# A hybrid attention layer: the pacing count is zeroed with each change of pace, and the latent heads and first output products take a background step at every third tile

## The chip, the core and the metric

The kernel runs on one core of a Trainium2 chip. The metric is device time in microseconds for one execution, lower is better; the time before is the median of three runs. One execution was also recorded by the hardware profiler, and all durations in this document come from that record.

## What is computed

One layer with two groups of eight heads each. The latent heads (MLA, "m") take queries, keys and values from two normalised latent vectors of 768 and 512 columns, with a rotary part; the forgetting heads (FoX, "f") take them from the input directly and add a cumulated log of a forget gate to the scores. Both outputs are gated, joined, projected and normalised.

```python
h = _rms_norm(x, g_pre)                       # x: 512 tokens x 2048
proj = h @ w_in                               # all first projections in one matrix
q_lat, kv_lat, k_rope_raw, gate_mla, fq, fk, fv, f_logit, gate_fox = jnp.split(proj, ...)
o_mla = _mla_branch(q_lat, kv_lat, k_rope_raw, g_q, w_uq, g_kv, w_ukv, cos, sin) * silu(gate_mla)
o_fox = _fox_branch(fq, fk, fv, f_logit, b_forget) * silu(gate_fox)
o = jnp.concatenate([o_mla, o_fox], axis=-1) @ w_out
return x + _rms_norm(o, g_post)
```

Every matrix is float32. The kernel splits each operand into a high and a low part and multiplies three times (high by high, high by low, low by high; `mm3`, L137 to L140).

## The kernel before

**Chunks and tiles.** Weights come in chunks of at most 128 x 1024 float32 (512 KB), in an order fixed when the program is written down. `chunk(i)` issues the loads on SyncE's queue (SP) up to chunk i+4 (`load`, L221 or L230, into one of three `raw` buffers), and divides up to chunk i+2 (`divide`, L242 and L243: ScalarE copies `whi`, VectorE subtracts `wlo`; three buffers of each). A chunk is used in two or four *tiles*: one slice of 128 rows, with 6 or 9 matmuls of 512 columns, or as many columns in narrower ones.

**Stages, in order.** Forgetting heads in four pairs; one chunk group for the last latent columns (`lat`, 16 tiles); the other latent columns ("l") and the latent heads' gate ("m") as block products; the latent heads in four pairs (`for p in range(4)`, each with 6 tiles of w_uq and 4 of w_ukv); the output projection as block products, last the norm. While one pair of heads is projected, the scores and values of the pair before are put in between, taken from a queue `todo` (`pump`), one or two at each tile.

**Block products.** The gate, the latent columns and both halves of the output projection use seven products in place of eight of half the size (a Strassen-like scheme, `p1 p2 p4 q6 g5 g7 g3`). Four of the seven multiply not blocks of the weights but sums of blocks, t4 to t7. Each product has four chunks and eight tiles. The order for the output half is p1 (columns 0), p1 (columns 1), p2 (0), p4 (0), p4 (1), q6 (0), g5 (0) and so on, so that the first sums are used in the fourth product.

**The background sums.** The sums are made in DRAM while other work runs. The list `bg` has 64 entries: 32 for w_in, then 32 for w_out (16 for each half; their tensors are t4 to t7 and stand as `t` in the profile where a second number was in the name). `add_step(n, mark)` (L281 to L292) does three things: on GpSimd's queue (POOL) a DMA that adds the second block onto entry n-1 (L287), on SP's queue a DMA that copies the first block into entry n (L290), and on SP's queue a *mark* of 64 bytes from the current chunk's `whi` into the head of entry n+1 (L292). The mark holds the copy of the next step back: copy n+1 writes over the place where mark n+1 has to land first, and the mark itself can't start before that `whi` is written. The addition waits for its copy, and a load of a sum waits for its addition. A `whi` buffer can be written again only when the mark that reads it is through.

**The pace.** `paced(w)` is called once per tile. It counts `state["tiles"]` up, and where the count has reached `state["pace"]` it takes the pace off the count and does one step. There are 66 steps, from -1 to 64. The pace is 6 at the start, 4 for `lat` (L1172), 1000 from the first block products on (L1238, no steps meant), 6 from product g5 of the gate (L1291), 2.5 from the latent heads (L1305) and 4 from the output products (L1473). Only the pace is set at these places; the count runs on. Ahead of the output's product p4 stands `assert state["step"] > len(bg)`.

**Who waits for whom.** Each engine and each queue works in order. SP's queue carries the loads of chunks, the copies, the marks, and the fetches of activations parked in DRAM (L892); a copy that waits for its mark holds back all loads behind it. The order within a queue is set when the program is built.

Of the kernel before, what the change touches and what calls it, by code (L numbers as in the profile page):

```python
# [63 lines left out]
def tile_hybrid_layer(  # L64
# [30 lines left out]
    def slot(name, dt=F32, shape=(P, 2, S)):  # L95

        return sp.tile(list(shape), dt, tag="s", name=name)
# [4 lines left out]
    def proj_bank(name):  # L102
        return bank("pj", name, 4)
# [142 lines left out]
    state = {"loaded": 0, "divided": 0, "tiles": 0, "turn": 0, "step": -1, "pace": 6}  # L246
# [217 lines left out]
            todo.popleft()()  # L464

    later = deque()

    def paced(w):

        if state["step"] <= len(bg):  # L470
            state["tiles"] += 1
            if state["tiles"] >= state["pace"]:
                state["tiles"] -= state["pace"]
                add_step(state["step"], w[0:1, 0, 0:16].bitcast(F32))
                state["step"] += 1
# [432 lines left out]
    def operand(n, of):  # L908
        def parts(kk, t):
            return [oper[n, of][kk // 2][:, x, kk % 2, t * P : (t + 1) * P] for x in range(2)]  # L910

        return parts

    def product(name, g, parts, o, first, last, rate=1, at=None, held=0, side=(), turned=False):


        side = deque(side)
        kk = 0

        def step(j, kk, t, hi, lo):  # L920
            if not turned:
                mm3(
                    o[t], *parts(kk, t), hi[:, j, :], lo[:, j, :], first and kk == 0, last and kk == 7,
                    skip_group_check=True,
                )
                return
            for f in range(2):
                c = slice((2 * t + f) * P, (2 * t + f + 1) * P)
                mm3(
                    o[t][:, f * HALF : (f + 1) * HALF], hi[:, j, c], lo[:, j, c], *parts(kk),  # L930
                    first and kk == 0 and f == 0, last and kk == 7, skip_group_check=True,
                )

        rng = list(prods[name, g])
        for i in rng[: len(rng) - held]:
            hi, lo = chunk(i)
            for j in range(2):
                if at is not None and kk == at[0]:
                    at[1]()
                for t in range(2):  # L940
                    step(j, kk, t, hi, lo)
                kk += 1
                pump(rate)
                paced(hi)
                if side and not held and kk % 2 == 0:
                    side.popleft()()
        w = [chunk(i, ahead=0) for i in rng[len(rng) - held :]]
        if w:
            side.popleft()()
        for t in range(2):  # L950
            for m in range(2 * len(w)):
                step(m % 2, kk + m, t, *w[m // 2])
            if w:
                finish(t, 2, o[t])
# [84 lines left out]
    for p in range(4):  # L1039
# [18 lines left out]
        else:  # L1058
# [5 lines left out]
            if "v" in c:  # L1064
                n = 2 if p == 1 else 3
# [103 lines left out]
        latents[i] = split(raw(i), f"ln{i}")  # L1169

    todo.append(rotary_key)
    state["pace"] = 4  # L1172
    lb = [proj_bank(f"l4{i}") for i in range(2)]
    proj_T(lat, [(lb[i], P, two[i]) for i in range(2)], hh, hl)
    while later:
# [38 lines left out]
    def scaled(to, o, t0, add, op=ALU.add, col=hcol):  # L1214

        for t in range(2):
            dve.scalar_tensor_tensor(
                out=to[:, t, :], in0=o[t], scalar=col[:, t0 + t : t0 + t + 1], in1=add[:, t, :], op0=ALU.mult, op1=op
            )
# [5 lines left out]
    def gate(f, top, bottom):  # L1225

        if f % 2 == 0:
            o_of.append(slot(f"gm{f // 2}"))
        g = o_of[-1][:, f % 2, :]
        pt = att_bank(f"gmt{f}")  # L1230
        c = slice(f % 4 * P, (f % 4 + 1) * P)
        for t in range(NT):
            pe.transpose(pt[:, t * P : (t + 1) * P], (top, bottom)[t // 2][:, t % 2, c], ident)
        act.activation(g, pt, AF.Tanh)
        dve.scalar_tensor_tensor(out=g, in0=g, scalar=1.0, in1=pt, op0=ALU.add, op1=ALU.mult)
        gm.append(g)

    state["pace"] = 1000  # L1238
    A, A2 = ([proj_bank(f"g{n}{t}") for t in range(2)] for n in "lm")
    product("p1", "l", x_wide(0, 0), A, True, True, turned=True)  # L1240
    pl = slot("lp")
# [46 lines left out]
    product("q6", "m", operand("q6", "m"), C, True, True)  # L1288
    c12 = slot("gc12")
    scaled(c12, C, 0, pa, ALU.subtract)  # L1290
    state["pace"] = 6  # L1291
    product("g5", "m", operand("g5", "m"), G, True, True)
    c22 = slot("gc22")
    scaled(c22, G, 2, pb, ALU.subtract)
# [7 lines left out]
    todo.append(lambda: scaled(c12, G, 0, c12))  # L1302
    for f in range(4, 8):
        todo.append(lambda f=f: gate(f, c12, c22))
    state["pace"] = 2.5  # L1305
    for n in ("a11", "a12"):
        for f in fetches(n, "o"):
            f()
# [161 lines left out]
            square(t0 + t, c, o[t])  # L1470
            gain(t0 + t, c, o[t], homes.get(t0 + t))

    state["pace"] = 4  # L1473
    gps = [slot(f"gp{c}") for c in range(2)]

    def load_gp(c):
# [116 lines left out]
```

## Time and profile before

| | us |
|---|---|
| three runs | 961.98, 968.43, 968.26 |
| median | 968.26 |
| the profiled execution, device time | 962.62 |
| its span | 960.8 |

The profiled execution is 0.64 us above the lowest of the three runs and 5.64 below their median. TensorE (PE) is busy for 95% of the span. The profile's page cuts the span into 40 slices of 24.0 us and gives the busy share of each engine in tenths. The window view gives busy time, the number of instructions, the granted clock of TensorE as a share of full speed (PEclk), the mean busy share of the 16 DMA engines, and GB/s moved, for chosen stretches. The views of waits give who waited for whom: us in total, times, longest. Matmuls overlap: one of 512 columns takes 0.39 us and the next starts after less, so that the distance of two starts is what a matmul costs.

The stages in the trace, by the first start of their matmuls: `lat` 406.2, block products from 434.1, gate products q6 547.5, g5 560.1, g7 572.1; head pair 0 of the latent heads 631.5, pair 1 671.8, pair 2 about 713, pair 3 about 751; output products from 786.2, p4 from 832.4.

### The profile page before, as it was taken

How to read it: one execution, taken by the hardware profiler on the slowest of the kernel's cores; microseconds unless marked ns; L12 is line 12 of the kernel's file. 1: busy time of each engine (PE TensorE's matmuls, PEld its weight loads, DVE VectorE, ACT ScalarE, POOL GpSimd, SP SyncE). 2: the span in 40 equal slices, each digit the busy share in tenths (PEclk: the TensorE clock that was granted, in tenths of full speed). 3: DMA queues.
4: the chain of work that ended last, by engine and by line, in shares of the span. 5: the costliest groups of instructions: out<-in, count | busy, mean ns of one | idle time of the engine just before them, and what ended most of it. 6: DMA issues, size and time to landing. Idle time of an engine off the chain costs nothing.

```text
span 960.8 us, 12945 instructions
## 1 busy us (share of the span) xinstructions
PE 912.9 (95%) x4732; PEld 781.3 (81%) x4732; DVE 619.3 (64%) x1066; ACT 424.4 (44%) x779; POOL 87.5 (9%) x105
## 2 busy tenths in 40 slices
PE   8999999999999999999999995568899999999997
PEld 8988888988899888889999973347788888888885
DVE  4476886476634935737566775327588797796685
ACT  6762423243223422425645543214344456554474
POOL 0011101111200201111000001121100000000012
PEclk9999999999999999999999997689899999999999
DMA  9387988988988989897777689999921324777768
GB/s 291 86 234 200 233 207 224 226 202 226 255 200 216 214 233 246 206 219 254 241 243 250 191 255 246 250 262 246 233 78 35 107 89 155 239 232 242 263 200 248
DMA packets 122532, 203.60 MB, mean 212 GB/s; under 512 B 16194, under 2 KB 59740, under 8 KB 122468
## 3 DMA queue, kind: packets, MB, share of 16 engines
q1 hardware_dynamic: 105060, 158.85, 52.7%
q0 software_dynamic: 16672, 43.52, 24.2%
q8 instruction: 37, 0.61, 0.3%
q10 hardware_dynamic: 736, 0.40, 0.1%
q14 instruction: 27, 0.22, 0.1%
HBM read 190.66 MB, written 79.19 MB: 281 GB/s over the span
## 4 chain that ended last, share of the span: by engine, by line
PE 84%; DMA 12%; DVE 2%; SPq 1%; ACT 1%; issue 0%; ACTq 0%; DVEq 0%
DMA t<-whi 5%; PE fv L545 4%; DMA raw<-in_w_uq_dram 4%; PE fg L138 3%; PE fq L140 3%; PE fq L138 3%; PE fq L139 3%; PE fg L140 3%; PE fg L139 3%; PE fk L139 3%; PE fk L140 3%; PE fk L138 3%; PE sm L588 2%; PE fv L140 2%; PE fv L139 2%; PE fv L138 2%
## 5 line engine op out<-in xcount | busy, mean ns | idle before, releaser
L243 DVE TENSOR_TENSOR wlo<-raw,whi 128x1024 fp32r<-128x1024 f32 (+3 forms) x205 | 242.9, 1186 | 223.8 <-ACT whi L242 213.6
L242 ACT CAST whi<-raw 128x1024 fp32r<-128x1024 f32 (+3 forms) x205 | 209.4, 1022 | 337.2 <-PE fk L139 48.5
L138 PE MATMUL fq<-h,whi 128*128 128x512 f32 x128 | 52.6, 411 | 0.0
L138 PE MATMUL fg<-h,whi 128*128 128x512 f32 x128 | 50.9, 398 | 0.0
L140 PE MATMUL fq<-h,wlo 128*128 128x512 f32 x128 | 50.3, 393 | 0.0
L140 PE MATMUL fg<-h,wlo 128*128 128x512 f32 x128 | 50.1, 392 | 0.0
L139 PE MATMUL fq<-h,whi 128*128 128x512 f32 x128 | 50.1, 391 | 0.0
L138 PE MATMUL fk<-h,whi 128*128 128x512 f32 x128 | 50.0, 391 | 0.0
L139 PE MATMUL fg<-h,whi 128*128 128x512 f32 x128 | 49.9, 390 | 0.0
L139 PE MATMUL fk<-h,whi 128*128 128x512 f32 x128 | 49.8, 389 | 0.0
L140 PE MATMUL fk<-h,wlo 128*128 128x512 f32 x128 | 49.8, 389 | 0.0
L138 PE MATMUL mq<-ln,whi 128*128 128x512 f32 x72 | 30.6, 425 | 10.3 <-ACT whi L242 8.4
L140 PE MATMUL fv<-whi,h 128*128 128x256 f32 (+1 forms) x128 | 39.5, 309 | 0.0
L139 PE MATMUL fv<-wlo,h 128*128 128x256 f32 (+1 forms) x128 | 39.5, 309 | 0.0
L138 PE MATMUL fv<-whi,h 128*128 128x256 f32 (+1 forms) x128 | 39.5, 309 | 0.0
L545 PE MATMUL fv<-whi,h 128*128 128x456 f32 x128 | 37.7, 378 | 0.0
L287 POOL DMA_DIRECT2D t<-in_w_out_dram x16 | 19.4, 1302 | 154.9 <-DMA t<-in_w_out_dram 142.5
L139 PE MATMUL mq<-ln,whi 128*128 128x512 f32 x72 | 29.6, 411 | 0.0
L140 PE MATMUL mq<-ln,wlo 128*128 128x512 f32 x72 | 29.5, 413 | 0.0
L1409 POOL DMA_DIRECT2D c<-in_x_dram x8 | 7.1, 963 | 238.9 <-ACT c L1408 238.7
L605 ACT ACTIVATE pf<-sf,stf 128x128 f32<-128x128 f32 (+3 forms) x32 | 16.9, 528 | 26.9 <-DVE stf L603 26.9
L140 PEld LDWEIGHTS fq<-h,wlo 128*128 128x128 f32 x128 | 24.0, 188 | 5.4
(526 smaller groups left out, 2485.0 us busy)
## 6 DMA issues: line engine op xcount, KB each, us to landing
raw<-in_w_in_dram SPq DMA_DIRECT2D x80, 512.0 KB
t<-in_w_out_dram SPq DMA_DIRECT2D x32, 512.0 KB
raw<-t SPq DMA_DIRECT2D x32, 512.0 KB
raw<-in_w_out_dram SPq DMA_DIRECT2D x24, 512.0 KB
t<-in_w_out_dram POOLq DMA_DIRECT2D x16, 512.0 KB, 11.2
t<-t POOLq DMA_DIRECT2D x16, 512.0 KB, 8.1
awaymg<-rmg POOLq DMA_DIRECT2D x8, 512.0 KB, 7.7
raw<-in_w_ukv_dram SPq DMA_DIRECT2D x8, 512.0 KB
```

The costliest lines, as they stand in the source:

```text
L138: pe.matmul(o, ah, bh, start=first, stop=False, **kw)
L139: pe.matmul(o, ah, bl, start=False, stop=False, **kw)
L140: pe.matmul(o, al, bh, start=False, stop=last, **kw)
L242: act.copy(hi[:, :m], raw[:, :m])
L243: dve.tensor_tensor(out=lo[:, :m], in0=raw[:, :m], in1=hi[:, :m].bitcast(F32), op=ALU.subtract)
L287: pool.dma_start(to.rearrange("p (k c) -> p k c", k=2), second, accum_op=ALU.add)
L545: pe.matmul(banks[t][:, :n], a[k][:, tss[t]], b[:, j, :], start=k == 0 and m == 0, stop=k == NK - 1 and m == 2,)
L588: pe.matmul(s[:, :nn], a[:, qs], c[:, :nn], start=(i == 0), stop=(i == len(pairs) - 1))
L605: act.activation(p, s[:, :n], AF.Exp, bias=st[:, 0:1], accum_out=st[:, 1:2])
L1409: pool.dma_start(to, x[piece(t, c)], accum_op=ALU.add)
```

## The change

A helper sets the pace and the count together, and all changes of pace use it. The latent heads' pace goes from 2.5 to 3, that of the output products from 4 to 3.

```diff
     later = deque()
+
+    def set_pace(n):
+        state.update(pace=n, tiles=0)
...
-    state["pace"] = 4
+    set_pace(4)
     lb = [proj_bank(f"l4{i}") for i in range(2)]
...
-    state["pace"] = 1000
+    set_pace(1000)
     A, A2 = ([proj_bank(f"g{n}{t}") for t in range(2)] for n in "lm")
...
-    state["pace"] = 6
+    set_pace(6)
     product("g5", "m", operand("g5", "m"), G, True, True)
...
-    state["pace"] = 2.5
+    set_pace(3)
     for n in ("a11", "a12"):
         for f in fetches(n, "o"):
             f()
...
-    state["pace"] = 4
+    set_pace(3)
     gps = [slot(f"gp{c}") for c in range(2)]
```

No other line differs. What is computed, and every buffer, stays as it was.

## The prediction

> **What bounds the kernel now.** I read the page first. TensorE (PE) has work nearly everywhere, so time can be gained only where it has none.
>
> ```profile
> span 960.8 us, 12945 instructions
> PE   8999999999999999999999995568899999999997
> PE 84%; DMA 12%; DVE 2%; SPq 1%; ACT 1%; issue 0%; ACTq 0%; DVEq 0%
> ```
>
> The second line is PE's busy share in 40 slices of 24 us: one dip, 5 5 6 8 8, from about 600 us on. The third is the chain of waits that ended last: 84% PE, and 12% of the span (some 115 us) DMA. I cut that region by stages with the window view (columns: PE, weight load, VectorE, ScalarE and GpSimd busy with counts, granted clock, DMA share, GB/s):
>
> ```profile
> 406.00:434.00 28.00, 28.00 (x139) 23.18 (x138) 11.39 (x16) 8.83 (x16) 2.84 (x3) 1.00 0.92 213
> 572.00:631.00 59.00, 35.72 (x112) 24.90 (x111) 27.66 (x37) 17.50 (x23) 11.07 (x11) 0.74 1.01 248
> 631.00:672.00 41.00, 29.21 (x147) 23.40 (x146) 21.47 (x31) 13.71 (x27) 6.82 (x7) 0.92 1.06 263
> 672.00:713.00 41.00, 37.28 (x195) 31.80 (x194) 28.19 (x63) 17.64 (x45) 2.85 (x3) 0.92 0.72 175
> 713.00:751.00 38.00, 38.00 (x219) 32.81 (x217) 31.84 (x68) 19.38 (x50) 0.00 (x0) 1.00 0.20 60
> 751.00:786.00 35.00, 35.00 (x204) 30.78 (x203) 29.77 (x64) 17.59 (x43) 0.00 (x0) 1.00 0.23 76
> 786.00:805.00 19.00, 19.00 (x102) 15.83 (x100) 17.57 (x45) 12.09 (x31) 0.00 (x0) 1.00 0.36 112
> 805.00:822.00 17.00, 17.00 (x86) 14.01 (x85) 9.13 (x13) 9.92 (x17) 0.00 (x0) 1.00 0.62 199
> 822.00:832.00 10.00, 10.00 (x47) 8.30 (x46) 6.97 (x8) 5.43 (x8) 0.00 (x0) 1.00 0.87 292
> 832.00:854.00 22.00, 22.00 (x99) 18.22 (x98) 21.21 (x29) 14.90 (x22) 0.00 (x0) 1.00 0.72 217
> ```
>
> The second to fourth rows (gate products g7 and g3, then head pairs 0 and 1) are the dip. PE is idle for 23.3, 11.8 and 3.7 us there, and its clock is down to 0.74 and 0.92. The DMA engines are full, at 1.01 and 1.06. Right behind, in pairs 2 and 3, PE is full and DMA stands at 0.20 and 0.23. Who waits for whom between 572 and 672 us:
>
> ```profile
> PE gcm L138 <- ACT whi L242: 11.3, 3, 7.4
> PE mq L138 <- ACT whi L242: 8.4, 1, 8.4
> PE gdm L138 <- ACT whi L242: 8.3, 2, 7.2
> ACT whi L242 <- DMA t<-whi: 24.4, 9, 7.1
> SPq L290 <- DMA t<-whi: 41.3, 7, 9.6
> ```
>
> PE waits for divided weights, 28.0 us in these three rows. ScalarE, which divides, waits 24.4 us until a mark has read its buffer. SP waits 41.3 us at L290 with the loads queued behind it. So the background steps starve PE there, by filling the DMA engines.
>
> **Why they stand there: the count.** By the code, the forgetting heads have 14 groups of 16 tiles (q, k and g of four pairs, v of two). 224 tiles at pace 6 make 37 steps and leave 2. `lat` adds 16 at pace 4: 4 steps, 2 left. Eleven products of 8 tiles at pace 1000 raise the count to 90. At pace 6 each tile then adds one and takes six off, so a step falls on each of 18 tiles, and one more on the 24th. With 41 done, 60 of 66 are out when the latent heads begin, and the other 6 take 15 tiles at 2.5. The copies end in pair 1, as they should by this count:
>
> ```profile
> L290 SPq DMA_DIRECT2D t<-in_w_out_dram x32: 557/558/4197, 354.6 to 682.5; - x32
> 554.28 0.24 SPq L292 DMA_DIRECT2D t<-whi  x1
> 577.05 0.73 PE L138 MATMUL gcm<-whi,bmg 128*128 128x512 f32 x2 [1.41 <-ACT whi L242]
> ```
>
> (First row: min, median and max issue time in ns, then first and last start.) After the change `lat` still has 4 steps, each 2 tiles later, 41 in all. Then come 4 in products g5, g7 and g3 (24 tiles at 6), 13 in the latent heads (40 tiles at 3), and 8 in p1, p1 and p2 of the output (24 at 3). That is 66, the last on the last tile before the assertion.
>
> **Part 1: what goes.** What the dip would take with PE fed, from distances between starts:
>
> ```profile
> 841.70 0.39 PE L140 MATMUL ob<-whi,soa 128*128 128x512 f32 x1
> 849.86 0.39 PE L140 MATMUL ob<-whi,soa 128*128 128x512 f32 x1
> 545.81 0.28 PE L139 MATMUL gdl<-bmg,whi 128*128 128x256 f32 x1
> 547.37 0.28 PE L140 MATMUL gdl<-bmg,wlo 128*128 128x256 f32 x1
> 608.98 0.60 PE L1233 MATMUL gmt<-ident,gc 128*128 128x128 f32 x4
> PE mq L138 <- ACT mw L122: 1.9, 1, 1.9
> ```
>
> From 841.70 to 849.86 there are 36 distances: 0.227 us per matmul of 512 columns. From 545.81 to 547.37 there are 13: 0.12 us at 256. Products g7 and g3 have 16 tiles of 6: 96 x 0.227 = 21.8. Eight gates of four transposes: 8 x 0.60 = 4.8. Pair 0: 54 matmuls for w_uq and 24 for w_ukv, 78 x 0.227 = 17.7, and 48 narrow ones, 5.8. The wait for a bank in the last row, 1.9, stays. Sum 52.0 us, where the trace takes 572 to 672, 100 us: 48 gone. Pair 1 should take what pair 2 takes, 38 instead of 41: 3 more. **51 us** in all.
>
> That asks more of VectorE: 27.66 + 21.47 = 49.1 us of work in 52. Pair 2 runs with PE full at 31.84/38 = 0.84; at that share 49.1 us would need 58.6. So 0 to 6.6 us come back; I take **3**, about the middle, since neither end has a row that is nearer.
>
> **Part 2: what is added elsewhere.** The price of a step on the DMA engines, from the queues between 580 and 650 us:
>
> ```profile
> q1 hardware_dynamic: 8448, 11.08, 52.8%
> q0 software_dynamic: 2561, 6.56, 51.3%
> ```
>
> (Packets, MB, share of 16 engines.) 51.3% of 70 us for 6.56 MB of additions is 2.9 us for one of 0.524 MB. On SP's queue 52.8% for 11.08 MB is 1.75 us for 0.524 MB. So a step costs about 4.6 us of all engines, and a loaded chunk 1.75.
>
> *Gate products (4 steps).* 4 x 4.6 + 12 chunks x 1.75 = 39.4 us of DMA for 8 x 6 x 3 matmuls x 0.227 = 32.7 us of PE: 6.7 over. The nearest row is `lat` (first window row): 4 steps there, DMA at 0.92, no idle PE. And the bunched steps started at 554.28, but PE first went idle at about 577, 23 us later, because loaded and divided chunks stand ahead. The cost is 0 to 6.7; I take **2**.
>
> *Latent heads (13 steps).* 13 x 4.6 = 60 us over about 137 us (52.0 less the products' 26.6, then 38, 38 and 35): 0.44 on top of 0.2, so 0.65 of the DMA engines. Marks, copies and additions have room, and SP's loads too. If that cover were gone, ScalarE would wait for marks again, 24.4/9 = 2.7 us each, 35 us for 13. I take **1** (0 to 6, two such waits).
>
> *Output, p1, p1, p2 (8 steps).* Here is too little room. DMA work now is 0.36 x 19 = 6.8, 0.62 x 17 = 10.5 and 0.87 x 10 = 8.7 us. With 2, 3 and 3 steps it becomes 16.0 of 19, 24.3 of 17 and 22.5 of 10. So 7.3 + 12.5 = 19.8 us of transfers are late when p2 ends. Products p4 then leave 28% of 22 us, 6 us, to catch up. What queues behind: SP's copy waits for its mark and holds back loads of chunks; the last addition of the sums for p4 (1) is issued with the last tile of p2, and its load comes 8 tiles (11 us) later. The chunks loaded ahead carried PE for 23 us in the dip, so most of the lateness stays hidden. The cost is 0 to 19.8 us; I take **6**, nearer to the low end because of that row.
>
> A gain from DMA contention that ends elsewhere I leave out: outside these stages PE is full.
>
> **Sum.** 51 - 3 - 2 - 1 - 6 = 39 us off the profiled execution's 962.6: 923.6. The three runs shown lie at 961.98, 968.43 and 968.26, that is 0.6 below to 5.8 above this execution; I set the forecast at **925**. With each cost at its better end the profile would give 912, at its worse end 51 - 6.6 - 6.7 - 6 - 19.8 = 12 off, 951.
>
> **Rivals.**
>
> *The dip moves to the output products* (chance 0.2). All 19.8 us late reach PE, and the clock falls with it. For: the two overloaded rows above. Against: the 23 us of cover. The clock's price comes from here:
>
> ```profile
> 583.47 0.73 PE L138 MATMUL gcm<-whi,bmg 128*128 128x512 f32 x2 [2.56 <-ACT whi L242]
> 584.73 0.79 PE L139 MATMUL gcm<-wlo,bmg 128*128 128x512 f32 x1 [0.53 <-DVE wlo L243]
> ```
>
> In the window 572 to 631, 35.7 us busy at 0.74 lose 9.3 us to the clock over the five waits of gcm and gdm: 1.9 us each. Three such gaps add 5.7. Then 51 - 3 - 2 - 1 - 25.5 = 19.5, 943 us. The gap of 2.56 us above was already followed by a matmul of 0.79 us in place of 0.39. [...]
>
> *Slower: a mark holds a division wherever a step stands* (0.05). If each of the 25 steps, spread or not, kept ScalarE 2.7 us and PE with it, 68 us would stand against the 51: 17 slower, 980. It decides once more than 51/2.7 = 19 steps do so. Against: over the whole span that wait is no longer than in the dip alone, so the 41 steps before it have none. From the view of the marks' line, who waited for them:
>
> ```profile
>   ACT whi L242: 24.4, 9
> ```
>
> *The steps don't move* (0.05). SP's order is set at building; if copies were placed early again, or queued until the next stage, time stays at 962 to 968.
>
> *GpSimd's additions and VectorE block each other* (0.05). Additions now fall where VectorE is at 0.84 beside a full PE:
>
> ```profile
> L287 POOL DMA_DIRECT2D t<-in_w_out_dram x16: 1128/1165/1898, 362.4 to 678.4; - x16
> L607 DVE TENSOR_SCALAR pf<-pf,stf x32: 275/378/487, 102.6 to 399.6; 128x128 f32<-128x128 f32 x8, 128x256 f32<-128x256 f32 x8, 128x384 f32<-128x384 f32 x8, 128x512 f32<-128x512 f32 x8
> ```
>
> 13 of them at 1.17 us, each holding VectorE on the path, add 15 us: 939. [...] The trace speaks against a price: the softmax scaling L607 ran beside steps in the forgetting heads and never took over 487 ns, for its widest form.
>
> **The numbers.** My forecast has 0.65: 912 to 934. The rivals have 0.2 (935 to 950), 0.05 (980), 0.05 (962 to 968) and 0.05 (939). Cutting 5% off below and the two cases on top, 0.1, and widening for the unknown output cost gives **910 to 947**. One per cent, 9.7 us, is about what a measurement tells from no change. Faster by more: 0.65 + 0.2 + 0.05 = 0.9, less a little for the tails: **0.89**. Within: **0.06**. Slower: **0.05**.
>
> **What would show it.** Copies (L290) of `t` spread from the gate products to the end of p2, the last about 4 us ahead of p2's last tile. No PE wait for `whi` over 3 us in g7, g3 and pair 0; DMA about 0.65 in the latent heads; pair 0 beginning near 600 us and the output products near 740. ScalarE's 24.4 us for marks gone or under 5. In p2 and p4, DMA near 1.0 and PE idle for some 6 us. The forecast is wrong if pair 0 and pair 1 still take over 70 us together, or if PE is idle for over 15 us from p1 on.

## The result

The changed kernel takes 926.36 us (median of 6, 922.60 to 928.72), the kernel before 966.69 in the same comparison (median of 6): the ratio is 0.9581, with a 95% interval of 0.9549 to 0.9614. 925 was forecast. The profiled execution took 925.18 us, its span 923.4, that is 37.4 less than the span before.

The profile after, line for line with that of before (the page's span, PE in 40 slices of 23.1 us, the chain that ended last):

```profile
span 923.4 us, 12965 instructions
PE   9999999999999999999999999889999989999997
PE 86%; DMA 7%; DVE 4%; ACT 2%; issue 1%; SPq 0%; ACTq 0%; DVEq 0%
```

The dip is gone but for two slices of 8; a new 8 stands where the output products begin. DMA in the chain fell from 12% to 7%. The window view of the changed kernel, cut at its own stages (gate products g7 and g3; head pairs 0, 1, 2, 3; p1, p1 and p2 of the output; p4; the rest), has the columns of the view before:

```profile
572.00:599.00 27.00, 24.27 (x112) 19.51 (x111) 25.31 (x35) 16.07 (x22) 2.29 (x3) 1.00 0.98 266
599.00:631.00 32.00, 28.87 (x148) 24.26 (x147) 23.76 (x36) 14.15 (x27) 3.35 (x4) 0.89 0.85 217
631.00:665.00 34.00, 33.63 (x190) 29.08 (x189) 26.62 (x59) 17.11 (x44) 3.95 (x4) 1.00 0.88 204
665.00:703.00 38.00, 37.97 (x220) 32.84 (x219) 31.82 (x67) 19.58 (x52) 3.14 (x3) 1.00 0.64 150
703.00:738.00 35.00, 35.00 (x203) 30.73 (x204) 29.81 (x64) 17.47 (x45) 3.10 (x3) 1.00 0.67 167
738.00:790.00 52.00, 48.24 (x235) 40.20 (x234) 33.37 (x65) 26.91 (x53) 4.80 (x5) 0.97 0.84 238
790.00:817.00 27.00, 24.58 (x100) 17.86 (x99) 21.13 (x28) 15.64 (x24) 0.81 (x1) 1.00 0.79 257
817.00:923.00 106.00, 99.80 (x436) 81.22 (x434) 75.00 (x111) 56.06 (x83) 9.60 (x10) 0.99 0.79 243
```

The first three rows are 93 us; the same work took 141 (572 to 713) before. PE is idle there for 2.7, 3.1 and 0.4 us in place of 23.3, 11.8 and 3.7. Pairs 2 and 3 take 38 and 35 us as before, now with DMA at 0.64 and 0.67 in place of 0.20 and 0.23: there the moved steps cost nothing. The next two rows lose: p1 to p4 take 79 us by these cuts, 68 before.

The copies run almost to the end of p2 (column: first and last start), and VectorE's softmax scaling beside them keeps its median of 382 ns (min, median, max in ns):

```profile
L290 SPq DMA_DIRECT2D t<-in_w_out_dram x32: 557/558/1235, 357.2 to 779.9; - x32
```

```profile
L610 DVE TENSOR_SCALAR pm<-pm,stm x32: 276/382/523, 639.2 to 762.9; 128x128 f32<-128x128 f32 x8, 128x256 f32<-128x256 f32 x8, 128x384 f32<-128x384 f32 x8, 128x512 f32<-128x512 f32 x8
```

Two waits stand out. Who waits in the changed kernel from 572 to 672 us, and then from 738 to 813 (total, times, longest):

```profile
ACT boa L129 <- DMA boa<-awayoa: 5.0, 3, 2.2
PE gmt L1236 <- DVE gm L1238: 3.1, 1, 3.1
PE mq L138 <- ACT gm L1237: 1.6, 1, 1.6
```

```profile
ACT whi L242 <- DMA raw<-t: 10.1, 4, 5.2
ACT boa L129 <- DMA boa<-awayoa: 5.0, 1, 5.0
PE sm L591 <- ACT pm L608: 3.8, 1, 3.8
PE ob L139 <- DVE wlo L243: 2.0, 3, 0.8
```

No PE wait for a first `whi` is left in the first list, and no ScalarE wait for a mark. In their place ScalarE waits for `boa`: parked head outputs that are fetched from DRAM over SP's queue. It does so in pair 0 and in the output's first product, 5.0 us in all each time, and PE then stands for 3.1 and for 3.8 us, for something queued behind that on ScalarE. In the output's first product the fetch was issued right behind a background copy (timeline of SP in the changed kernel):

```profile
741.03 0.56 SPq L290 DMA_DIRECT2D t<-in_w_out_dram  x1
741.70 1.02 SPq L895 DMA_DIRECT2D boa<-awayoa  x2
```

In pair 0 four fetches were issued from 598.30 us on, behind two loads of w_ukv (594.89 and 597.83) and, ahead of these, a copy (591.67).

### The profile page after: what moved, and what is told of

The parts are those of the page before. It is cut to its first block, busy times and chain, and to the rows that moved or that the text cites. A ratio compares the mean times of both kernels' runs of the same rounds, so it can differ in the third digit from the quotient of the medians.

```text
span 923.4 us, 12965 instructions
## 1 busy us (share of the span) xinstructions
PE 902.2 (98%) x4732; PEld 775.7 (84%) x4732; DVE 619.2 (67%) x1066; ACT 424.2 (46%) x779; POOL 87.2 (9%) x105
## 4 chain that ended last, share of the span: by engine, by line
PE 86%; DMA 7%; DVE 4%; ACT 2%; issue 1%; SPq 0%; ACTq 0%; DVEq 0%
PE fv L548 4%; PE fg L138 3%; PE fq L140 3%; PE fq L138 3%; PE fq L139 3%; PE fg L140 3%; PE fg L139 3%; PE fk L140 3%; PE fk L139 3%; PE fk L138 3%; DMA raw<-t 2%; PE fv L140 2%; PE fv L139 2%; PE fv L138 2%; DMA boa<-awayoa 2%; PE sm L591 2%
## 5 line engine op out<-in xcount | busy, mean ns | idle before, releaser
L140 PE MATMUL fv<-whi,h 128*128 128x256 f32 (+1 forms) x128 | 39.5, 309 | 0.0
L139 PE MATMUL fv<-wlo,h 128*128 128x256 f32 (+1 forms) x128 | 39.5, 309 | 0.0
L138 PE MATMUL fv<-whi,h 128*128 128x256 f32 (+1 forms) x128 | 39.5, 309 | 0.0
L608 ACT ACTIVATE pm<-sm,stm 128x128 f32<-128x128 f32 (+3 forms) x32 | 16.9, 528 | 27.6 <-DVE stm L606 27.6
```

The source lines that it names most:

```text
L138: pe.matmul(o, ah, bh, start=first, stop=False, **kw)
L139: pe.matmul(o, ah, bl, start=False, stop=False, **kw)
L140: pe.matmul(o, al, bh, start=False, stop=last, **kw)
L608: act.activation(p, s[:, :n], AF.Exp, bias=st[:, 0:1], accum_out=st[:, 1:2])
```

## The experiments

The table has the stages of all kernels, as distances of the first starts of their matmuls in each profiled execution. The medians of the kernel before in these comparisons are 965.68 (first four), 966.79 (next four) and 965.66 (last two). The profiled execution of zeroing alone was the longest of its four, 4.6 us above their median (919.83 us); which of its stages hold this excess is not known.

| kernel | median, us | ratio to before (95%) | g5 to pair 0 | four pairs | p1, p1, p2 | p4 | rest |
|---|---|---|---|---|---|---|---|
| before | 966.69 | | 71.4 | 154.6 | 46.2 | 21.8 | 106.6 |
| the change | 926.36 | 0.9581 (0.9549 to 0.9614) | 38.5 | 139.9 | 51.6 | 26.5 | 106.8 |
| zeroing alone | 915.19 | 0.9488 (0.9449 to 0.9527) | 39.5 | 140.3 | 46.3 | 21.8 | 106.7 |
| new paces alone | 964.52 | 0.9982 (0.9955 to 1.0008) | 73.4 | 154.3 | 46.2 | 21.8 | 106.7 |
| before, thin additions | 927.13 | 0.9605 (0.9576 to 0.9635) | 55.2 | 136.4 | 46.3 | 21.8 | 106.7 |
| latent pace 2 | 924.46 | 0.9573 (0.9527 to 0.9618) | 39.5 | 148.6 | 46.1 | 21.8 | 106.7 |
| a22 fetched early | 921.22 | 0.9533 (0.9503 to 0.9562) | 39.2 | 139.1 | 46.6 | 27.1 | 107.0 |
| output pace 2.6 | 924.34 | 0.9567 (0.9535 to 0.9600) | 38.2 | 138.7 | 51.5 | 25.2 | 106.9 |
| zeroing, a11 and a12 early | 915.05 | 0.9466 (0.9442 to 0.9490) | 40.5 | 135.4 | 46.2 | 21.8 | 106.7 |
| zeroing, 4 steps moved | 909.87 | 0.9414 (0.9390 to 0.9438) | 36.9 | 135.0 | 46.2 | 21.8 | 106.7 |
| the change, t5 last | 925.72 | 0.9589 (0.9560 to 0.9617) | 39.1 | 137.0 | 56.1 | 25.2 | 106.7 |
| zeroing, moved, a11 and a12 early | 909.13 | 0.9415 (0.9387 to 0.9443) | 37.3 | 134.1 | 46.2 | 21.8 | 106.7 |

### Which half of the change does it

Zeroing alone, against the changed kernel:

```diff
-    set_pace(3)
+    set_pace(2.5)
     for n in ("a11", "a12"):
...
-    set_pace(3)
+    set_pace(4)
     gps = [slot(f"gp{c}") for c in range(2)]
```

> The count is zeroed at each change of pace, but the latent heads keep 2.5 and the output products 4. By the code: 41 steps, then 4 in the gate products, 16 in the latent heads, 5 in p1, p1, p2 of the output. Theory (the zeroing alone spreads the steps, the new paces add nothing to it): the latent heads end about 48 us earlier than before, as in the changed kernel; with 5 in place of 8 steps in the output products about half of the 10 us lost there returns: 918 to 924 us. Rival (the paces of 3 are what keeps the loads on time): 16 steps at 2.5 crowd the latent heads, time 935 us or more.

915.19 us: the theory, and 3 us better than its range. The latent heads and the output take 16 and 5 steps instead of 13 and 8, p1 to p4 are back at 68.1 us as before, and the latent heads have not grown. The window view of this kernel for p1, p1, p2 and for p4:

```profile
743.00:790.00 47.00, 47.00 (x235) 38.90 (x234) 33.94 (x66) 28.22 (x56) 2.78 (x3) 1.00 0.84 253
790.00:811.00 21.00, 21.00 (x95) 17.38 (x94) 20.50 (x28) 14.15 (x20) 0.00 (x0) 1.00 0.64 200
```

PE is never idle in them. DMA is at 0.84 in the first three products, as in the changed kernel, but over 47 us rather than 52.

The paces alone, against the kernel before:

```diff
-    state["pace"] = 2.5
+    state["pace"] = 3
...
-    state["pace"] = 4
+    state["pace"] = 3
```

> The two paces become 3, the count is not zeroed. By the code 60 steps are still out when the latent heads begin, and the other 6 take 18 tiles in place of 15. Theory (the count carried over makes the dip): as before, 960 to 968 us, PE idle for over 20 us between 572 and 631 us. Rival (the paces do a share of it): 950 us or less.

964.52 us, and the interval includes no change from before. The window view of this kernel has the same dip:

```profile
572.00:631.00 59.00, 35.94 (x110) 24.61 (x109) 29.30 (x39) 16.67 (x22) 7.92 (x8) 0.74 1.01 248
```

So the zeroing makes the whole gain. The new paces move nothing while the count runs on, and once it is zeroed they cost 926.36 less 915.19, 11 us (9 us by the two ratios).

### Volume or marks

Against the kernel before:

```diff
         if n > 0:
             to, _, second = bg[n - 1]
-            pool.dma_start(to.rearrange("p (k c) -> p k c", k=2), second, accum_op=ALU.add)
+            c = 64 if n > 40 else 512
+            to = to.rearrange("p (k c) -> p k c", k=2)
+            pool.dma_start(to[:, :, :c], second[:, :, :c], accum_op=ALU.add)
```

> The kernel before, steps bunched as they were, but from entry 40 of the list on the additions move 64 of 512 columns; the other columns of those sums lack their second block. Marks, copies and the order of the queues stay. Theory (the volume of transfers starves PE): a step costs the DMA engines 1.75 us for the copy and 0.4 for the addition in place of 4.6, 19 steps and 12 chunks 61 us in place of 108 for 33 us of PE, so that with some 15 us of cover 30 to 40 of the 51 us go: 925 to 937 us. Rival (each step's mark holds SP's queue and ScalarE, whatever the volume): 955 us or more, and ScalarE still waits over 15 us for marks.

927.13 us, inside the theory's range: with seven eighths of the additions' bytes gone, and marks and queues as they were, the stages from g5 to the output shrink from 226.0 to 191.6 us, 34 of the 47.6 that the change takes off them. ScalarE's wait for marks between 572 and 672 us falls with them, from 24.4 us to

```profile
ACT whi L242 <- DMA t<-whi: 11.0, 7, 2.9
```

The volume of transfers starves PE; more than half of the wait for marks was a wait for the transfers ahead of them. Pair 0 still comes 55.2 us after g5, not 39 as with spread steps: bunched copies with thin additions fill the DMA engines too, as the window view of this kernel has it:

```profile
572.00:601.00 29.00, 20.97 (x75) 14.30 (x73) 23.01 (x34) 13.54 (x19) 7.92 (x7) 0.88 0.97 248
601.00:627.00 26.00, 20.96 (x90) 15.48 (x91) 10.10 (x11) 8.15 (x10) 8.28 (x8) 1.00 1.02 272
```

### Room in the latent heads

Against the changed kernel:

```diff
-    set_pace(3)
+    set_pace(2)
     for n in ("a11", "a12"):
```

> The changed kernel with pace 2 in the latent heads: 20 steps there, 1 in the output products, in place of 13 and 8. Theory (the 10 us lost after the latent heads come from the 8 steps beside p1, p1, p2): the output products start at most 5 us later than in the changed kernel, DMA at about 0.9 in the latent heads, and p1 to p4 take 68 us as in the kernel before in place of 78: 916 to 922 us. Rival (the latent heads have no room for 20): what is gained in the output is lost there, 925 us or more.

924.46 us, between the two. The table shows why: the output returns to 67.9 us, 10.2 gained, and the four pairs take 148.6 us, 8.7 more. The window view of this kernel for the end of pair 0 and for pair 1 (635.8 to 676.5 us):

```profile
627.00:662.00 35.00, 31.98 (x158) 26.93 (x157) 22.47 (x51) 14.06 (x35) 5.92 (x6) 0.90 0.99 231
662.00:702.00 40.00, 39.62 (x230) 34.31 (x229) 33.76 (x73) 19.75 (x50) 6.02 (x6) 1.00 0.98 224
```

With DMA at 0.99, PE is idle for 3.0 us and its clock falls to 0.90. In pair 1 ScalarE waits 6.9 us for one chunk of w_ukv. The output's loss is the steps beside it, as the theory had it; but the latent heads do not take 20 for nothing, as the rival had it. With 16 (zeroing alone) they take about as long as with 13: 140.3 us against 139.9.

### The loss in the output: a fetch, a deadline, or volume

Fetching a22 early, against the changed kernel:

```diff
     for p in range(4):
         c = mla[p]
+        if p == 3:
+            for f in fetches("a22", "o"):
+                f()
...
-    product("p1", 0, operand("a11", "o"), A, True, True, 2, side=fetches("a22", "o"))
+    product("p1", 0, operand("a11", "o"), A, True, True, 2)
```

> The changed kernel, with the two fetches of block a22 issued at the start of head pair 3 in place of the output's first product. In the changed kernel ScalarE waits 5.0 us at about 746 to 751 us for such a fetch, queued behind a copy, and PE then stands for 4.15 us. Theory (that wait is 4 of the 10 us lost in the output): no idle PE over 1 us in p1, p1 and p2, these three take 46 to 48 us in place of 51.6, time 920 to 923. Rival (the DMA engines are late anyway, and another wait takes its place): the three products still take over 50 us, time as in the changed kernel.

921.22 us, as the theory had it: p1, p1 and p2 take 46.6 us, and the wait of PE for `pm` is gone. (The intervals of this kernel and of the changed one overlap a little; the reading rests on the stages.) In the changed kernel the wait stands so, first on ScalarE (start, us, and in brackets the idle time before), then on PE:

```profile
751.11 0.62 ACT L129 CAST boa<-boa 128x512 fp32r<-128x512 f32 x1 [5.00 <-DMA boa<-awayoa]
751.64 0.58 ACT L608 ACTIVATE pm<-sm,stm 128x384 f32<-128x384 f32 x1
```

```profile
752.36 0.82 PE L591 MATMUL sm<-mk,mq 128*128 128x256 f32 x3 [3.76 <-ACT pm L608]
```

The softmax step of 751.64 stood behind the division of `boa`, though its own input was there: VectorE's reduction for it began at 745.95 and took 0.56 us. p4 stays at 27.1 us, so its 5 us are another matter. For them I had a deadline in mind, since SP in the changed kernel waits at the load of the last sum (waits of SP, 738 to 813 us):

```profile
SPq L221 <- DMA t<-t: 10.1, 1, 10.1
```

The same steps, ended earlier, against the changed kernel:

```diff
-    set_pace(3)
+    set_pace(2.6)
     gps = [slot(f"gp{c}") for c in range(2)]
```

> The changed kernel with pace 2.6 in the output products: the same steps, the last three tiles (4 us) earlier. Theory (p4's stall is a deadline: the load of the last sum holds SP's queue until its addition has landed, 6.6 to 10 us in the changed kernel): SP's wait there and p4's idle PE shrink, p4 takes 23 to 25 us in place of 26.5, time 922 to 925. Rival (it is the volume of transfers, whenever they stand): p1 to p4 take as long as in the changed kernel, 78 us, time within 2 us of it.

924.34 us and p4 at 25.2: SP's wait halves to 5.0 us, p4 gets 1.3 us back, but the 51.5 us ahead of it stay. The time fits both expectations and settles nothing. So the last sum was made another one, against the changed kernel:

```diff
                 bg.append((W[name, g][j], first, second))
+        if g == 1:
+            at = len(bg) - 16
+            order = [4 * j + n for a in (0, 2) for n in (0, 2, 3) for j in (a, a + 1)]
+            bg[at:] = [bg[at + i] for i in order + [1, 5, 9, 13]]
```

> The changed kernel, with the list of sums for the second output half in another order: t7, t6 and t4 of two chunks at a time, the four t5 at the end. Paces, steps and transfers stay; the last sum of product p4 is now entry 59 of 0 to 63, 12 tiles earlier. Theory (deadline: p4 loses 4.8 us because SP's queue waits for the addition of its last sum): SP's wait for that addition under 2 us, p4 takes 22 to 23 us in place of 26.5, time 3 to 5 us below the changed kernel's. Rival (volume: 8 steps beside p1, p1, p2 make the loads late): p4 still takes 25 us or more.

925.72 us: the rival, if by little. The row of SP's wait for an addition is gone from the same view, and p4 still takes 25.2 us, 3.4 above the kernel before, where the rival asked for 25 or more. ScalarE waits there for chunks that have been issued but have not landed:

```profile
ACT whi L242 <- DMA raw<-t: 8.6, 3, 4.2
```

```profile
780.00:790.00 10.00, 10.00 (x48) 8.30 (x47) 6.04 (x8) 5.80 (x9) 1.13 (x1) 1.00 1.06 292
790.00:813.00 23.00, 21.09 (x89) 16.10 (x88) 16.36 (x22) 11.43 (x17) 1.13 (x1) 1.00 0.81 272
```

(Waits and windows of this kernel, p2 and p4.) p2 ends with the DMA engines at 1.06, and p4 pays. The deadline was there, but not what p4's time hung on alone. That p1 to p2 grew to 56.1 us in this order fits the same kind of wait, a second time: ScalarE waits 4.8 us for `boa` up to 748.75 and 4.4 us for another parked fetch, `boq`, up to 769.52, and PE is idle for 3.54 us ahead of 749.99 and for 1.83 ahead of 772.21; the mean granted clock is 0.86 from 738 to 763 us and 0.90 from 763 to 780. No run with these fetches moved was made for this order.

### What is left of the dip

The fetches of a11 and a12 earlier, against zeroing alone:

```diff
+    for n in ("a11", "a12"):
+        for f in fetches(n, "o"):
+            f()
     product("g7", "m", operand("g7", "m"), C, False, True)
...
     set_pace(2.5)
-    for n in ("a11", "a12"):
-        for f in fetches(n, "o"):
-            f()
```

> The kernel with zeroing alone (2.5 and 4), with the fetches of blocks a11 and a12 issued ahead of gate product g7 in place of after g3. In the changed kernel and in that one ScalarE waits some 5 us in head pair 0 for these fetches, the gates behind it are late, and PE stands for 3.5 us and then runs at half clock. Theory (that wait is what is left of the dip): no idle PE over 2 us in pair 0, clock 1.0 there, 4 to 7 us off: 908 to 911. Rival (the DMA engines are full in the gate products, and four more transfers there starve PE of chunks): waits for divided weights return in g7 or g3, 914 us or more.

915.05 us, as without the edit. ScalarE's wait for `boa` in pair 0 is gone, and the four pairs are 4.9 us shorter than in the profiled execution of zeroing alone; but ahead of pair 0 stands a wait of PE that is 3.5 us long in place of 1.0. Waits of this kernel, 595 to 720 us:

```profile
PE gmt L1236 <- DVE gc L1220: 3.5, 1, 3.5
ACT whi L242 <- DMA raw<-in_w_uq_dram: 3.0, 1, 3.0
```

One wait took the place of the other: the time lies in the rival's range, but neither theory had named this wait. Taking the four steps out of the gate products instead, against zeroing alone:

```diff
     drain()
+    set_pace(10)
     C, G = ([proj_bank(f"g{n}l{t}") for t in range(2)] for n in "cd")
...
-    set_pace(6)
+    set_pace(1000)
     product("g5", "m", operand("g5", "m"), G, True, True)
```

> The kernel with zeroing alone, but its 4 steps of the gate products g5, g7, g3 stand in the five block products ahead of them (pace 10 over 40 tiles, then none until the latent heads). Theory (the gate products are over their DMA budget by 7 us, at a cost of about 2 us, and their lateness makes the fetches of pair 0 late): DMA share in 572 to 601 us falls from 0.9 to about 0.65, ScalarE's wait for the fetches shrinks, time 909 to 913. Rival (the four steps cost PE nothing where they are): time within 2 us of the kernel with zeroing alone, 913 to 917.

909.87 us, 5.3 below zeroing alone (7 by the two ratios). The window view of this kernel, first the products that took the steps, then the gate products, which lost them, and pairs 0 and 1:

```profile
501.00:524.00 23.00, 23.00 (x186) 22.61 (x185) 16.26 (x18) 11.93 (x15) 1.20 (x1) 1.00 0.90 285
524.00:547.00 23.00, 23.00 (x194) 23.00 (x193) 16.31 (x19) 11.77 (x15) 0.88 (x1) 1.00 0.90 280
...
572.00:601.00 29.00, 27.44 (x129) 22.53 (x128) 28.80 (x41) 17.29 (x23) 0.00 (x0) 1.00 0.59 165
601.00:627.00 26.00, 25.20 (x141) 21.31 (x140) 21.77 (x33) 14.18 (x27) 2.78 (x3) 1.00 0.91 232
627.00:662.00 35.00, 34.63 (x198) 29.75 (x196) 28.08 (x61) 18.02 (x47) 5.11 (x5) 1.00 0.98 240
```

The earlier products run at 0.90 of the DMA engines with PE full. In the gate products the share is 0.59, PE is idle for 1.6 us there and for 0.8 in pair 0, and the clock stays at full speed. Pair 1 runs at 0.98 and loses next to nothing. With both edits:

> The kernel with zeroing alone and the 4 steps moved ahead of the gate products, and besides the fetches of a11 and a12 issued ahead of product g7. Theory (what is left in head pair 0, 1 to 2 us of idle PE, is the wait of 1.9 us for these fetches): 907 to 909 us. Rival (nothing of it is on the path any more): as without it, 909 to 911 us.

909.13 us (908.50 to 911.14), against 909.87 (909.15 to 911.13): no difference that these runs tell, as the rival had it. It and the kernel with the four steps moved are the fastest here, 17 us below the change.

## Why the prediction was right

**The cause of the dip** was the count carried over: the two halves of the change show it. That the steps starve PE by their volume more than by their marks is shown by the thin additions.

**The count of steps.** As worked out from the code: 4, 13 and 8 steps. One detail was off. The last copy starts at 779.9 us, 10 us ahead of p2's end at 790 and so some 9 us ahead of its last tile, not 4. By the code, a step's copy is held by its mark alone, and the order set at building puts it as soon as that is through, so copies run up to a step ahead of their tile.

**Part 1, 51 us less 3 for VectorE, 2 for the gate products and 1 in the latent heads: 45.** The output products start at 738.6 us in place of 786.2: 47.6. Pair 0 begins at 598.6 (forecast near 600). The parts were less exact than their sum. From g7 (572.1) to pair 1 (630.7) the changed kernel takes 58.6 us, where the sum had 52 and the 3 and 2 us. The kernel with the four steps moved takes 52.1 us there (573.8 to 625.9), with the same divisions on VectorE: so VectorE's 3 us were not needed, and what the changed kernel loses is the fetch that holds ScalarE, with the low clock behind it (0.50 from 611.2 to 614 us), and the four steps: 6.5 us between these two profiles. Moving the steps gave 5.3 us by the medians, from zeroing alone. The fetch was not in the sum, though the waits of the kernel before, 572 to 672 us, have it:

```profile
ACT boa L129 <- DMA boa<-awayoa: 4.0, 2, 3.0
```

Pair 1, set at the 38 us of pair 2, takes 34.7; it has fewer matmuls (197 records, pair 2 has 218). These 3.3 us more than make up for the rest.

**The latent heads, 1 us.** Right in cost for pairs 1 to 3, wrong in share: 0.85 and 0.88 of the DMA engines in pairs 0 and 1, not 0.65, and 0.64 and 0.67 in pairs 2 and 3. Work that was late from the gate products does not explain it: with the four steps moved, and 16 in the latent heads, the share is 0.91 and 0.98 there. The margin was smaller than the step said: 16 steps took about as long as 13, 20 cost 9 us more.

**The output, 6 us in a range of 0 to 19.8.** Measured: 51.6 less 46.2 and 26.5 less 21.8, 10.1 us. This term was the mis-sized one. 5 us of it come from a wait that the prediction had not looked for: a fetch of parked activations, stuck behind a copy, that holds ScalarE and with it the softmax. The other 5 are late chunks in p4, behind a p2 in which the DMA engines stood at 1.07 (780 to 790 us); with 5 steps or 1 beside p1 to p2 p4 takes 21.8 us again. The late addition that the prediction named beside it is not needed for 3.4 of these 5 us. That PE is idle for 6.2 us from p1 to p4, as the prediction said of p2 and p4, is luck: 3.8 of them stand in p1, for the fetch.

**The sum.** 39 us were forecast, 37.4 measured on the profiled executions: 1.6 short, because the dip gave 2.6 more and the output took 4.1 more. The mechanism was right; that the time came within 2 us of the forecast is in part luck, since these errors, and those within the dip, nearly cancel.

**The rivals.** The dip did not move whole: 10 of 25.5 us. Marks hold no division in the changed kernel: ScalarE has no wait for one from 440 to 960 us. A few scalings on VectorE took longer beside an addition that GpSimd issued, by 0.1 us in the changed kernel and in the kernel before. The longest scaling of L610 in the changed kernel, 523 ns, began while GpSimd issued an addition:

```profile
643.93 1.13 POOL L287 DMA_DIRECT2D t<-in_w_out_dram  x1 [10.95 <-DMA raw<-in_w_uq_dram]
644.29 0.52 DVE L610 TENSOR_SCALAR pm<-pm,stm 128x384 f32<-128x384 f32 x1
```

The other scalings of the latent heads in this form take 409 to 423 ns. In the kernel before it is the 587 ns of 693.07 us, beside the last addition (692.86); the others of its form take 475 to 487. The longest in any run is 741 ns, in the kernel with a22 fetched early, at 645.42 beside an addition of 645.20. Of the latent heads' scalings in the changed kernel only two met an addition's issue, one without delay, and the price there is 0.1 us; no run shows the 1.17 us for each of 13 that the rival had. A maximum over all widths, as the prediction used, hides such a delay in the narrower forms. The clock is taken up below.

## What to carry to other kernels

A pacing counter that is compared with a changed limit has to be reset, or its backlog comes out as one burst where the limit falls. Give background transfers to each stage by its own share of the DMA engines, and look at what is queued in order behind them: here a small fetch on the same queue held ScalarE for 5.0 us while it had other work ready. `lat` at 0.92 of the DMA engines, and block products with the moved steps at 0.90, ran with PE full here. Nearer to 1 the share alone did not decide: pair 1 took 34.7 us at 0.98 with 16 steps in the latent heads and the gate products relieved, and 40.7 at 0.98 to 0.99 with 20, where one chunk came late; p2 ran full at 1.07 and p4 paid, 26.5 us in place of 21.8.

## What the runs showed of the hardware

TensorE's granted clock fell to 0.50 at short idle times. In the changed kernel it did so at a gap of 3.13 us (timeline of PE: idle before in brackets, then the next matmuls; those of 512 columns took 0.39 to 0.40 us from 601.5 to 604 us, at a clock of 1.00):

```profile
610.39 1.12 PE L1236 MATMUL gmt<-ident,gc 128*128 128x128 f32 x4 [3.13 <-DVE gm L1238]
611.15 0.78 PE L140 MATMUL mq<-ln,wlo 128*128 128x512 f32 x1
611.73 0.63 PE L138 MATMUL mq<-ln,whi 128*128 128x512 f32 x1
```

From 611.2 to 614 us the granted clock is 0.50. The kernel before showed it after 2.56 us, ahead of 583.47: the clock is 0.50 from 584.5 to 587 us.

In these runs the length of one gap did not decide it alone. In the kernel with t5 last, the clock fell after 1.83 us (0.51 from 772.9 to 775.8); in the kernel before with thin additions it stayed at 1.00 after 2.75 us (602.9 to 606.5):

```profile
772.21 0.47 PE L138 MATMUL pvm<-phm,mv3h 128*128 128x512 f32 x1 [1.83 <-ACT whi L242]
772.99 0.63 PE L138 MATMUL oa<-whi,soa 128*128 128x512 f32 x1
```

```profile
602.91 0.72 PE L138 MATMUL gdm<-whi,bmg 128*128 128x512 f32 x2 [2.75 <-ACT whi L242]
604.51 0.40 PE L140 MATMUL gdm<-whi,bmg 128*128 128x512 f32 x1
```

The kernel with the four steps moved has 1.6, 0.8 and 0.4 us of idle PE in the three windows from 572 to 662 us, and its granted clock is 1.00 in each.
